# Expert routing in a two-layer decoder: tokens fetched from HBM by index instead of one-hot matmuls

## The chip, the cores and the metric

The kernel runs on one core of a Trainium2 chip (trn2). The metric is the device time of one execution in microseconds (us), lower is better. PE is the matrix engine, PEld its weight loads, DVE the vector engine, ACT the scalar engine, POOL the GpSimd engine and SP the engine whose queue issues most DMAs.

## What is computed

Two layers of a decoder over 256 tokens of width 1024. Layer 0 has a recurrent block, sparse attention, cross-attention and a dense SwiGLU; layer 1 has a state-space mixer, cross-attention and a top-2-of-8 expert SwiGLU. Only the last part is touched:

```
def moe(h, router, w13, w2):
    logits = (h @ router).astype(jnp.float32)
    top_v, top_i = lax.top_k(logits, TOP_K)
    w = jax.nn.softmax(top_v, axis=-1)
    gate = jnp.sum(jax.nn.one_hot(top_i, N_EXPERTS) * w[..., None], axis=-2)
    y = jnp.zeros_like(h)
    for e in range(N_EXPERTS):
        y = y + gate[..., e:e + 1] * swiglu(h, w13[e], w2[e])
    return y
```

Here h is the RMS-normed x (256 tokens by 1024), w13[e] is 1024 by 7168 and w2[e] is 3584 by 1024, all in f32. The result is added to x.

## The kernel before

**Routing.** In `mo_open` the logits give each token two experts. `mo["pos"]` holds, for every token and expert, the token's place among that expert's tokens (1000 is added where it was not chosen), and `mo["gate"]` its weight. An expert works on 128 places. If any expert has more than 128 tokens, a branch at the end (`overflow`) does the rest; it is not entered here.

**Weights.** Each expert has 42 weight pieces of 128 by 2048 f32 (1 MB): 28 of w13 and 14 of w2. The class `Stream` loads them in a fixed order on SP's queue (L208), into 14 buffers in several pools (raw, kv, hl, m_yy). A piece is split in two halves of 1024 columns: ACT copies a rounded high part `wh` (L222), DVE subtracts for the low part `wl` (L225). There are three buffers of `wh` and `wl`. A product is three matmuls, high by high, high by low and low by high (L431, L432, L433). When a piece has been split, its load buffer is free and SP issues the next load.

**Expert loop.** For each expert e and each of seven column blocks c, the steps are four pieces of w13 (`mo_up`, i = 0 to 3, 12 matmuls each), with the transposes of the previous block's hidden values (`mo_tr`, L2029) after i = 0, and then two pieces of w2 for the previous block (`mo_w2`, 12 matmuls each). The end of an expert's w2 therefore falls into block c = 0 of the next expert, where `mo_comb` stands.

**Tokens into an expert.** After (c, i) = (1, 3) `onehot` builds a 0/1 matrix `mo_D` (tokens by places) for the next expert. `x3` holds the normed tokens as three bf16 parts that add up to f32. In blocks 2 to 5, after i = 1 and i = 3, `gather` runs for one of eight column groups k: six bf16 matmuls of 128 columns (L1987), an ACT copy with the norm's gain (L1992) and a DVE subtraction (L1993), into `mo_x0` or `mo_x1` in turn.

**Outputs back to tokens.** After (6, 2) `onehot_T` transposes `mo_D` (two PE transposes, L2003; one ACT copy, L2005). `mo_comb` splits the expert's output from PSUM (two ACT copies, two DVE subtractions, L427 and L428). One and two heavy steps later four pairs of 512-column matmuls (L2066, L2067) bring it back into token order, and DVE adds it to X with the gate as factor (L2069, four times). For the last expert this is the tail of the kernel, with `dump` storing X.

The order of the work on each engine is the order in which the code issues it.

Of the kernel before, what the change touches and what calls it, by code (L numbers as in the profile page):

```python
# [22 lines left out]
D = 1024  # L23
# [79 lines left out]
def pack(inp):  # L103
    a = {k: np.asarray(v) for k, v in inp.items()}
    out = {"x": a["x"][0], "mem": a["mem"][0]}
    par = np.zeros((128, NP_), np.float32)

    def put(k, v):
        par[:, POFF[k][0]:POFF[k][1]] = v
    for l in range(2):  # L110
        for n in ("mix", "cross", "mem", "ffn"):
            put(f"{n}{l}", _cols(a[f"norm_{n}"][l]))
    put("rgw", _cols(a["ev_rg_conv_w"][0]))
    put("rgb", _cols(a["ev_rg_conv_b"][0]))
# [12 lines left out]
    out["cst"], out["cstb"] = _consts()  # L127
    out["grow"] = np.stack([a["norm_mix"][0], a["norm_cross"][0], a["norm_ffn"][0], a["norm_mix"][1],
                             a["norm_cross"][1]])
    out["row"] = np.concatenate([a["od_dt_bias"][0], a["od_a_log"][0], a["od_d_skip"][0],  # L130
                                 a["ev_nsa_gate_b"][0]])[None]
    w_in, od_in = a["ev_w_in"][0], a["od_w_in"][0]
    small = np.concatenate([w_in[:, 4608:4632], od_in[:, 5120:5152], a["moe_router"][0]], 1)
    out["small"] = small.reshape(8, 128, 64).transpose(1, 0, 2).reshape(128, 512)
    out["cw2"] = np.concatenate([a["ev_cmp_k_w2"][0].reshape(2, 128, 128).transpose(1, 0, 2),
                                 a["ev_cmp_v_w2"][0].reshape(2, 128, 128).transpose(1, 0, 2)], 1).reshape(128, 512)
    u = {}
    u["rgx"] = _blocks(w_in[:, 0:1024], 8, 256)
# [27 lines left out]
    return {k: np.ascontiguousarray(v) for k, v in out.items()}  # L166
# [122 lines left out]
def _program(ctx, nc, tc, d, upto):  # L289
# [22 lines left out]
    cstb = dp.tile([128, NB_], BF, name="cstb")  # L312
    sy.dma_start(cst[:, :128], d["cst"][:, :128])
    row = dp.tile([128, 120], F32, name="row")
    gmoe = cp.tile([128, 32], F32, name="gmoe")[:, :8]

    def load_consts():
        sy.dma_start(cst[:, 128:], d["cst"][:, 128:NCK])
# [1569 lines left out]
    def mo_open():  # L1888
# [100 lines left out]
    def gather_out(e, k, ps):  # L1989
# [5 lines left out]
    def gather(e, k):  # L1995
        ps = misc()
        gather_mm(e, k, ps, range(6))
        gather_out(e, k, ps)

    def onehot_T(e):  # L2000
        ps = mo["misc"].tile([128, 1024], BF, name="misc")
# [49 lines left out]
    def mo_comb(e):  # L2051
        def f1():
            oh, ol = (x.rearrange("p k c -> p (k c)").rearrange("p (n c) -> p n c", n=2) for x in mo["xg", e])
            for n in range(2):
                split_to(oh[:, n], ol[:, n], mo["po"][n])

            def f2(t):
                def f():
                    for n in range(2):
                        out(t, n)  # L2060
                return f

            def out(t, n):
                lw = mo["DT", e][:, t * 128:(t + 1) * 128]
                ps = misc()
                mm(ps, lw, oh[:, n], start=True, stop=False)  # L2066
                mm(ps, lw, ol[:, n], start=False, stop=True)  # L2067
                x = X[:, t, n * 512:(n + 1) * 512]
                ve.scalar_tensor_tensor(x, ps, mo["gate"][:, t, e:e + 1], x, op0=OP.mult, op1=OP.add)  # L2069
                if e == NE - 1:  # L2070
                    dump(t, n)
            if e < NE - 1:
                defer(1, f2(0))
                defer(2, f2(1))
            else:
                for n in range(2):
                    for t in range(2):
                        out(t, n)
        add(f1)

    def raw3():
        ST["S"].add_pool(ctx.enter_context(tc.tile_pool(name="raw3", bufs=NRAW3)), NRAW3)
# [1 line left out]
        ST["S"].finish()  # L2084
    add(raw3)
    add(mo_open)
    prev = None
    for e in range(NE):
        for c in range(7):
            for i, (kind, kh) in enumerate(((1, 0), (1, 1), (0, 0), (0, 1))):  # L2090
                mo_up(e, c, kind, kh)
                if i == 0 and prev is not None:
                    mo_tr(*prev)
                if e < 7 and (c, i) == (1, 3):
                    add(lambda e=e: onehot(e + 1))
                if e < 7 and 2 <= c < 6 and i % 2:
                    add(lambda e=e, k=2 * (c - 2) + i // 2: gather(e + 1, k))
                if (c, i) == (6, 2):
                    add(lambda e=e: onehot_T(e))
            if prev is not None:  # L2100
                final = (e, c) == (NE - 1, 6)
                for i in range(2):
                    if final and i:
                        add(lambda: ST["S"].limit(2))
                    mo_w2(*prev, i)
                if final:
                    mo_tr(e, c)
                    add(lambda: ST["S"].limit(3))
                if prev[1] == 6:
                    mo_comb(prev[0])  # L2110
            prev = (e, c)
    for i in range(2):
        mo_w2(*prev, i)
# [3 lines left out]
    def overflow():  # L2117
        n = nc.values_load(mo["cnti"][0:1, 0:1], min_val=0, max_val=256)
        MW.close()
        with tc.If(n > 128), tc.tile_pool(name="ovf", bufs=1) as op_:  # L2120
            D2 = op_.tile([128, 2, 128], BF, name="o_D")
            D2T = op_.tile([128, 256], F32R, name="o_DT")
            p2 = op_.tile([128, 2], F32, name="o_p")
            xg = op_.tile([128, 8, 128], F32, name="o_xg")
            sg = op_.tile([128, 512], F32, name="o_sg")
            hd = op_.tile([128, 512], F32, name="o_hd")
# [9 lines left out]
            for e in range(NE):  # L2136
# [6 lines left out]
                for k in range(8):  # L2143
                    ps = misc()[:, :128]
                    for i in range(6):
                        t, b = divmod(i, 3)
                        mm(ps, mo["x3"][b][:, t, k * 128:(k + 1) * 128], D2[:, t], start=i == 0, stop=i == 5)
                    sc.activation(xg[:, k], ps, AF.Copy, scale=gmoe[:, k:k + 1])
# [50 lines left out]
```

## Time and profile before

| | |
|---|---|
| median of 3 runs | 1796.58 us (1796.31 to 1799.18) |
| the profiled execution | 1799.66 us |
| its span in the profile | 1797.8 us, granted clock 0.989 |
| PE busy, instructions | 1739.1 us, 9381 |
| DVE, ACT, POOL busy | 1409.7, 1172.8, 311.5 us |
| moved by DMA | 478.63 MB, mean 266 GB/s |

The span is from the first to the last instruction; the execution's own time has about 2 us around it. The first expert begins at 802.77 us and the last matmul of all starts at 1788.43 us, so the expert stage is over half of the span. Matmuls overlap one another in the pipeline: the profile shows 0.39 us for one of 512 columns, while they start 0.23 us apart. The chain of waits counts each piece up to the start of the next and is what the times per matmul are read from.

### The profile page before, as it was taken

The numbers are of one execution on the slowest core, as the hardware profiler recorded it, in microseconds if no ns is written. First come the engines' busy times: TensorE is split into PE (matmuls) and PEld (weight loads), VectorE is DVE, ScalarE is ACT, GpSimd is POOL, SyncE is SP. The second block draws the span as 40 slices with busy tenths as digits, with TensorE's granted clock in tenths as the row PEclk, the third lists the DMA queues.
The fourth block names the chain that finished last, engine by engine and source line by source line (L and its number), as shares of the span: only waits on it lengthen the run. The fifth ranks groups of instructions, "written<-read, shape, count | busy, mean of one in ns | idle before, by whom it ended". The sixth has DMA issues, their size and how long they took to land.

```text
span 1797.8 us, 24661 instructions
## 1 busy us (share of the span) xinstructions
PE 1739.1 (97%) x9381; PEld 1453.1 (81%) x9384; DVE 1409.7 (78%) x1727; ACT 1172.8 (65%) x1686; POOL 311.5 (17%) x158
## 2 busy tenths in 40 slices
PE   7999999999998999989999999999999999999997
PEld 6797677899988787768888888888888888888885
DVE  6686756433358898568999899999999998999986
ACT  5646546544444655467787777777777777777774
POOL 4333132444435344230000000000000000000000
PEclk9999999999999999999999999999999999999999
DMA  8555243455563243559999999999999999999970
GB/s 302 214 213 188 85 161 120 181 174 187 193 218 119 99 158 109 232 209 350 358 369 352 352 355 363 362 348 355 361 359 357 368 353 356 357 360 366 356 304 26
DMA packets 71791, 478.63 MB, mean 266 GB/s; under 512 B 10864, under 2 KB 11376, under 8 KB 14448
## 3 DMA queue, kind: packets, MB, share of 16 engines
q1 hardware_dynamic: 67968, 474.36, 70.7%
q10 hardware_dynamic: 3696, 2.62, 0.5%
q8 instruction: 75, 1.23, 0.3%
q14 instruction: 52, 0.43, 0.1%
HBM read 475.90 MB, written 1.05 MB: 265 GB/s over the span
## 4 chain that ended last, share of the span: by engine, by line
PE 81%; DVE 11%; ACT 5%; issue 1%; DMA 1%; POOL 1%; SPq 0%; ACTq 0%; DVEq 0%; POOLq 0%
PE gu L431 11%; PE gu L433 11%; PE gu L432 11%; PE out L431 6%; PE out L433 6%; PE out L432 6%; PE acc L433 5%; PE acc L431 5%; PE acc L432 5%; PE aux L433 2%; PE aux L432 2%; PE aux L431 2%; DVE wl L225 1%; PE misc L2029 1%; PE misc L1987 1%
## 5 line engine op out<-in xcount | busy, mean ns | idle before, releaser
L225 DVE TENSOR_TENSOR wl<-raw,wh 128x1024 fp32r<-128x1024 f32 x619 | 746.3, 1243 | 136.6 <-ACT wh L222 132.5
L222 ACT ACTIVATE wh<-raw 128x1024 fp32r<-128x1024 f32 (+1 forms) x722 | 723.4, 1054 | 149.3 <-PE out L433 52.2
L225 POOL TENSOR_TENSOR wl<-raw,wh 128x1024 fp32r<-128x1024 f32 (+1 forms) x103 | 258.8, 2518 | 311.0 <-ACT wh L222 282.9
L431 PE MATMUL gu<-wh,mo_x0h 128*128 128x512 f32 x448 | 179.4, 400 | 0.0
L431 PE MATMUL gu<-wh,mo_x1h 128*128 128x512 f32 x448 | 179.0, 400 | 0.0
L431 PE MATMUL out<-wh,m_xsT 128*128 128x512 f32 x448 | 177.2, 396 | 0.7 <-ACT m_xsT L427 0.7
L433 PE MATMUL gu<-wh,mo_x0l 128*128 128x512 f32 x448 | 174.9, 390 | 0.0
L433 PE MATMUL gu<-wh,mo_x1l 128*128 128x512 f32 x448 | 174.9, 390 | 0.0
L433 PE MATMUL out<-wh,m_xsT 128*128 128x512 f32 x448 | 174.7, 390 | 0.0
L432 PE MATMUL gu<-wl,mo_x0h 128*128 128x512 f32 x448 | 174.7, 390 | 0.0
L432 PE MATMUL gu<-wl,mo_x1h 128*128 128x512 f32 x448 | 174.6, 390 | 0.0
L432 PE MATMUL out<-wl,m_xsT 128*128 128x512 f32 x448 | 174.4, 389 | 0.0
L431 PE MATMUL acc<-hh,wh 128*128 128x256 f32 x416 | 122.3, 294 | 0.7 <-DVE m_M L810 0.7
L432 PE MATMUL acc<-hl,wh 128*128 128x256 f32 x416 | 119.5, 287 | 0.5 <-DVE hl L428 0.5
L433 PE MATMUL acc<-hh,wl 128*128 128x256 f32 x416 | 119.1, 286 | 0.0
L432 PE MATMUL aux<-hl,wh 128*128 128x256 f32 x352 | 99.9, 284 | 1.3 <-DVE hl L428 1.3
L431 PE MATMUL aux<-hh,wh 128*128 128x256 f32 x352 | 99.8, 284 | 0.3 <-ACT hh L427 0.3
L433 PE MATMUL aux<-hh,wl 128*128 128x256 f32 x352 | 99.8, 283 | 0.0
L433 PEld LDWEIGHTS gu<-wh,mo_x0l 128*128 128x128 f32 x448 | 84.1, 188 | 18.6
L433 PEld LDWEIGHTS gu<-wh,mo_x1l 128*128 128x128 f32 x448 | 84.1, 188 | 18.5
L433 PEld LDWEIGHTS out<-wh,m_xsT 128*128 128x128 f32 x448 | 84.1, 188 | 18.4 <-DVE m_xsT L428 0.4
L431 PEld LDWEIGHTS out<-wh,m_xsT 128*128 128x128 f32 x448 | 84.1, 188 | 17.4 <-ACT m_xsT L427 0.9
(429 smaller groups left out, 3408.9 us busy)
## 6 DMA issues: line engine op xcount, KB each, us to landing
raw<-m SPq DMA_DIRECT2D x265, 1024.0 KB, 6.0
raw<-wd SPq DMA_DIRECT2D x110, 1024.0 KB, 4.8
m_yy<-m SPq DMA_DIRECT2D x24, 1024.0 KB, 6.0
kv<-m SPq DMA_DIRECT2D x24, 1024.0 KB, 5.8
hl<-m SPq DMA_DIRECT2D x23, 1024.0 KB, 5.7
X<-x SPq DMA_DIRECT2D x4, 256.0 KB, 5.1
raw<-wd SPq DMA_DIRECT2D x2, 512.0 KB, 8.3
rg_gw<-wd ACTq DMA_DIRECT2D x1, 1024.0 KB, 11.4
```

Of the source, the lines that this page charges most:

```text
L222: nc.scalar.activation(h[:, a:b], r[:, a:b], AF.Copy)
L225: (nc.gpsimd if eng else nc.vector).tensor_tensor(l[:, a:b], r[:, a:b], h[:, a:b].bitcast(F32), op=OP.subtract)
L431: mm(ps, wh, xh, start=first, stop=False)
L432: mm(ps, wh, xl, start=False, stop=False)
L433: mm(ps, wl, xh, start=False, stop=last)
L1987: mm(ps[:, :128], mo["x3"][b][:, t, k * 128:(k + 1) * 128], mo["D", e][:, t], start=i == 0, stop=i == 5)
L2029: pe.transpose(ps[:, j * 128:(j + 1) * 128], mo["hd", e, c][:, j * 128:(j + 1) * 128], ident)
```

## The change

Tokens and outputs go through HBM. After `mo_open`, the new step `normed` lets POOL multiply X by each token's norm factor and the gain, into f32 rows, and stores them in a DRAM tile `dx`. For experts 1 to 7 `gather_in` computes the token number of each of the 128 places (two matmuls with one column, `mo_D` as weights), and POOL issues an indexed DMA of 128 rows of 4 KB into the buffer `m_y`. After (4, 1) and (4, 3) `gather_tr` transposes them on PE, four transposes at a time, and splits the result as before in high and low part. Expert 0 is still gathered by one-hot matmuls inside `mo_open`.

For experts 0 to 6 `mo_store` takes the place of `mo_comb`: ACT copies the two output banks into SBUF, and POOL stores the 128 rows in the DRAM tile `do`. `choices` (15 small DVE operations in expert 0) computes where each token's two rows lie. In expert 7, after (2, 1) and (4, 1), `rows_out` fetches two rows per token by index for one half of the tokens, and after (4, 0) and (6, 0) `rows_add` adds them to X with their gates. Expert 7 itself keeps `onehot_T` and `mo_comb`.

```
+        for t in range(2):
+            gp.tensor_copy(rs_moe[:, t:t + 1], N["f1"].rs[t])
...
+    def normed():
+        g = m["o"].tile([128, D], F32, name="m_y")
+        gp.dma_start(g, d["grow"][5:6].to_broadcast([128, D]))
...
+        xn = hp.tile([128, 2, D], F32, name="hh")
+        mo["dx"] = dram.tile([T, D], F32, name="dx")
+        for t in range(2):
+            for c in range(2):
+                s = slice(c * 512, (c + 1) * 512)
+                gp.tensor_scalar(xn[:, t, s], X[:, t, s], rs_moe[:, t:t + 1], None, op0=OP.mult)
+                gp.tensor_tensor(xn[:, t, s], xn[:, t, s], g[:, s], op=OP.mult)
+            gp.dma_start(mo["dx"][t * 128:(t + 1) * 128], xn[:, t])
+
+    def rows_in(D_, tok, ix):
+        ps = misc()
+        for t in range(2):
+            mm(ps[:, :1], D_[:, t], tok[:, t:t + 1], start=t == 0, stop=t == 1)
+        ve.tensor_copy(ix, ps[:, :1])
+        rows = m["o"].tile([128, D], F32, name="m_y")
+        gp.indirect_dma_start(rows, None, mo["dx"][:, :], bass.IndirectOffsetOnAxis(ap=ix, axis=0))
+        return rows
...
+    def gather_tr(e, c):
+        ps = misc()
+        for j in range(4):
+            k = c * 4 + j
+            pe.transpose(ps[:, j * 128:(j + 1) * 128], mo["rows"][:, k * 128:(k + 1) * 128], ident)
+        xh, xl = (x[:, c * 4:c * 4 + 4].rearrange("p k c -> p (k c)") for x in mo["xg", e])
+        split_to(xh, xl, ps)
...
-            if e < NE - 1:
-                defer(1, f2(0))
-                defer(2, f2(1))
...
+    def mo_store(e):
+        def f():
+            if e == 0:
+                mo["st"] = hp.tile([128, 2, D], F32, name="hh")
+            o = mo["st"][:, e % 2]
+            for n in range(2):
+                sc.activation(o[:, n * 512:(n + 1) * 512], mo["po"][n], AF.Copy)
+            gp.dma_start(mo["do"][e * 128:(e + 1) * 128], o)
+        add(f)
...
+    def rows_out(t):
+        mo["back"] = [m["o"].tile([128, D], F32, name="m_y"),
+                      mo["st"][:, 1]]
+        for j in range(2):
+            gp.indirect_dma_start(mo["back"][j], None, mo["do"][:, :],
+                                  bass.IndirectOffsetOnAxis(ap=mo["ci"][:, j, t:t + 1], axis=0))
+
+    def rows_add(t):
+        for j in range(2):
+            ve.scalar_tensor_tensor(X[:, t], mo["back"][j], mo["cg"][:, j, t:t + 1], X[:, t],
+                                    op0=OP.mult, op1=OP.add)
...
-                if e < 7 and 2 <= c < 6 and i % 2:
-                    add(lambda e=e, k=2 * (c - 2) + i // 2: gather(e + 1, k))
-                if (c, i) == (6, 2):
+                if e < 7 and (c, i) == (2, 1):
+                    add(lambda e=e: gather_in(e + 1))
+                if e < 7 and c == 4 and i % 2:
+                    add(lambda e=e, h=i // 2: gather_tr(e + 1, h))
+                if (e, c, i) == (0, 3, 0):
+                    add(choices)
+                if (e, c, i) == (7, 6, 2):
                     add(lambda e=e: onehot_T(e))
+                if e == 7 and (c, i) in ((2, 1), (4, 1)):
+                    add(lambda t=c // 2 - 1: rows_out(t))
+                if e == 7 and (c, i) in ((4, 0), (6, 0)):
+                    add(lambda t=c // 2 - 2: rows_add(t))
...
-                    mo_comb(prev[0])
+                    mo_store(prev[0])
```

The change moves instructions, and three places show how (lines of the changed kernel are one to some tens higher). ACT in block c = 4 of expert 0, before; `wh` is a split, `mo_sg` a silu, `m_xsT` the copy after `mo_tr`, `mo_x0h` a gather copy:

```order
L427 ACTIVATE m_xsT<-misc 128x512
L222 ACTIVATE wh<-kv 128x1024 x2
L2019 ACTIVATE mo_sg<-gu 128x512
L1992 ACTIVATE mo_x0h<-misc,gmoe 128x128
L222 ACTIVATE wh<-raw 128x1024 x4
L1992 ACTIVATE mo_x0h<-misc,gmoe 128x128
L222 ACTIVATE wh<-raw 128x1024 x2
```

The same place in the changed kernel:

```order
L429 ACTIVATE m_xsT<-misc 128x512
L223 ACTIVATE wh<-kv 128x1024 x2
L2056 ACTIVATE mo_sg<-gu 128x512
L429 ACTIVATE mo_x1h<-misc 128x512
L223 ACTIVATE wh<-raw 128x1024 x4
L429 ACTIVATE mo_x1h<-misc 128x512
L223 ACTIVATE wh<-raw 128x1024 x2
```

Two copies of 512 columns stand where two of 128 stood; the six other small copies of blocks 2, 3 and 5 are gone. DVE in block c = 4 of expert 7, in the changed kernel (`X<-m_y` and `X<-hh` are `rows_add`):

```order
L2059 TENSOR_TENSOR mo_sg<-mo_sg,gu 128x512
L226 TENSOR_TENSOR wl<-raw,wh 128x1024 x6
L430 TENSOR_TENSOR m_xsT<-misc,m_xsT 128x512
L2150 SCALAR_TENSOR_TENSOR X<-m_y,mo_cg,X 128x1024
L2150 SCALAR_TENSOR_TENSOR X<-hh,mo_cg,X 128x1024
L226 TENSOR_TENSOR wl<-kv,wh 128x1024 x2
```

Two operations of 1024 columns stand between the splits there and once more in block 6; before, expert 7 had four of 512 columns in block 0. POOL, which has no instruction in the expert loop before, in the changed kernel from the start of the loop:

```order
L1994 TENSOR_TENSOR hh<-hh,m_y 128x512
L1995 DMA dx<-hh 128x1024
L1993 TENSOR_SCALAR hh<-X,gmoe 128x512
L1994 TENSOR_TENSOR hh<-hh,m_y 128x512
L1993 TENSOR_SCALAR hh<-X,gmoe 128x512
L1994 TENSOR_TENSOR hh<-hh,m_y 128x512
L1995 DMA dx<-hh 128x1024
L2003 DMA m_y<-dx,mo_ix 128x1024
L2114 DMA do<-hh 128x1024
L2003 DMA m_y<-dx,mo_ix 128x1024
L2114 DMA do<-hh 128x1024
```

Eight elementwise operations come first (four of each kind), then a fetch and a store in turn, seven of each, and four fetches in expert 7.

## Rows read from the trace of the kernel before

**Rows 1.** The page: busy times, and PE's busy tenths in 40 slices.
```profile
PE 1739.1 (97%) x9381; PEld 1453.1 (81%) x9384; DVE 1409.7 (78%) x1727; ACT 1172.8 (65%) x1686; POOL 311.5 (17%) x158
...
PE   7999999999998999989999999999999999999997
```

**Rows 2.** One window: length, busy us (count) by engine, clock, DMA share, GB/s.
```profile
830.00:1740.00 910.00, 910.00 (x4345) 743.38 (x4344) 837.37 (x836) 698.39 (x804) 0.00 (x0) 1.00 0.95 359
```

**Rows 3.** Groups by line and shape, 1000 to 1600 us.
```profile
L225 DVE TENSOR_TENSOR wl<-raw,wh 128x1024 fp32r<-128x1024 f32 x322 | 379.4, 1221 | 31.1 <-ACT wh L222 28.4
L222 ACT ACTIVATE wh<-raw 128x1024 fp32r<-128x1024 f32 x321 | 322.2, 1054 | 57.3 <-PE out L433 32.5 <-PE gu L433 24.8
L431 PE MATMUL gu<-wh,mo_x0h 128*128 128x512 f32 x288 | 115.2, 400 | 0.0
...
L427 ACT ACTIVATE m_xsT<-misc 128x512 fp32r<-128x512 f32 x34 | 20.4, 599 | 36.5 <-PE misc L2029 36.5
...
L2069 DVE SCALAR_TENSOR_TENSOR X<-misc,mo_gate,X 128x512 f32<-128x512 f32 x20 | 14.0, 743 | 0.0
```

**Rows 4.** Waits of SP's queue.
```profile
SPq L208 <- DVE wl L225: 1096.2, 374, 16.5
```

**Rows 5.** Chain, expert 2 (1041.9 to 1165.3 us): shares by line, one piece.
```profile
by line: PE gu L431 21.0%; PE gu L433 20.7%; PE gu L432 20.7%; PE out L431 10.5%; PE out L433 10.5%; PE out L432 10.3%; PE misc L2029 2.5%; PE misc L1987 2.3%; PE misc L2066 0.7%; PE misc L2067 0.7%; PE misc L2003 0.1%
...
1044.85 0.44 PE misc L2029 x4
```

**Rows 6.** Chain, pieces around one gather: start, us, what.
```profile
1013.10 0.23 PE gu L433
1013.33 0.35 PE misc L1987 x6
1013.68 0.29 PE gu L431
```

**Rows 7.** Chain, pieces around the transposes of `mo_tr`, expert 3.
```profile
1168.11 0.44 PE misc L2029 x4
1168.55 0.24 PE gu L431
```

**Rows 8.** Windows of 10 us in which DMA was nearly full.
```profile
730.00:740.00 10.00, 9.66 (x46) 7.57 (x45) 6.84 (x11) 5.48 (x8) 3.90 (x2) 1.00 0.99 415
...
860.00:870.00 10.00, 10.00 (x52) 8.16 (x51) 9.26 (x10) 6.67 (x8) 0.00 (x0) 1.00 0.98 343
...
930.00:940.00 10.00, 10.00 (x48) 8.29 (x47) 9.82 (x11) 8.13 (x10) 0.00 (x0) 1.00 1.00 397
...
1720.00:1730.00 10.00, 10.00 (x46) 8.29 (x45) 9.47 (x10) 7.48 (x8) 0.00 (x0) 1.00 0.99 396
```

**Rows 9.** Timeline: SP's last loads, ACT's last split.
```profile
1737.48 2.60 SPq L208 DMA_DIRECT2D raw<-m  x2
...
1779.19 2.00 ACT L222 ACTIVATE wh<-raw 128x1024 fp32r<-128x1024 f32 x2
```

**Rows 10.** A window of 10 us after the last load.
```profile
1750.00:1760.00 10.00, 10.00 (x46) 8.28 (x45) 9.41 (x10) 8.07 (x10) 0.00 (x0) 1.00 0.01 2
```

**Rows 11.** Timeline of DVE and POOL, 660 to 690 and 770 to 815 us.
```profile
661.68 2.53 DVE L1607 SCALAR_TENSOR_TENSOR m_xsT<-m_th,m_y 128x256 f32<-128x256 f32 x1
...
685.04 0.41 DVE L1607 SCALAR_TENSOR_TENSOR m_xsT<-m_th,m_y 128x256 f32<-128x256 f32 x1
...
773.60 3.49 DVE L225 TENSOR_TENSOR wl<-raw,wh 128x1024 fp32r<-128x1024 f32 x3
...
661.48 2.46 POOL L225 TENSOR_TENSOR wl<-raw,wh 128x1024 fp32r<-128x1024 f32 x1 [5.17 <-ACT wh L222]
...
667.49 3.03 POOL L1667 TENSOR_TENSOR m_y<-m_xs,row 128x512 f32<-128x512 f32 x2
...
773.73 5.56 POOL L225 TENSOR_TENSOR wl<-raw,wh 128x1024 fp32r<-128x1024 f32 x1 [6.80 <-ACT wh L222]
```

**Rows 12.** DMA issues of the page: size and us to landing.
```profile
raw<-m SPq DMA_DIRECT2D x265, 1024.0 KB, 6.0
```

More of the change, by code (lines that the diff above doesn't have):

```diff
@@ L15 @@
 I32 = mybir.dt.int32
+U32 = mybir.dt.uint32
 AF = mybir.ActivationFunctionType
@@ L128, in pack @@
     out["grow"] = np.stack([a["norm_mix"][0], a["norm_cross"][0], a["norm_ffn"][0], a["norm_mix"][1],
-                             a["norm_cross"][1]])
+                             a["norm_cross"][1], a["norm_ffn"][1]])
     out["row"] = np.concatenate([a["od_dt_bias"][0], a["od_a_log"][0], a["od_d_skip"][0],
@@ L314, in _program @@
     row = dp.tile([128, 120], F32, name="row")
-    gmoe = cp.tile([128, 32], F32, name="gmoe")[:, :8]
+    gm = cp.tile([128, 32], F32, name="gmoe")
+    gmoe, rs_moe = gm[:, :8], gm[:, 8:10]
     def load_consts():
@@ L1802, in _program @@
     mo = {}
+    dram = ctx.enter_context(tc.tile_pool(name="dram", bufs=1, space=bass.MemoryType.DRAM))
     add(mb_close2)
@@ L1973, in mo_open, with gather_in @@
         S.advance()
+    def normed():
+        g = m["o"].tile([128, D], F32, name="m_y")
+        gp.dma_start(g, d["grow"][5:6].to_broadcast([128, D]))
+        tk32 = mo["w2"].tile([128, 64], I32, name="mo_ti", bufs=1)[:, :2]
+        tk = mo["tok"] = mo["w2"].tile([128, 64], BF, name="mo_tok", bufs=1)[:, :2]
+        mo["ix"] = mo["w2"].tile([128, 32], U32, name="mo_ix", bufs=1)
+        gp.iota(tk32, pattern=[[128, 2]], base=0, channel_multiplier=1)
+        gp.tensor_copy(tk, tk32)
+        xn = hp.tile([128, 2, D], F32, name="hh")
[14 more added lines that the diff above has]
+        return rows
+    def gather_in(e):
+        mo["rows"] = rows_in(mo["D", e], mo["tok"], mo["ix"][:, e:e + 1])
+    def gather_tr(e, c):
[5 more added lines that the diff above has]
+        split_to(xh, xl, ps)
     def misc():
@@ L1993, in gather_out @@
         ve.scalar_tensor_tensor(xl[:, k], ps[:, :128], gk, xh[:, k].bitcast(F32), op0=OP.mult, op1=OP.subtract)
[L1995 to L1998, printed above, removed]
     def onehot_T(e):
@@ L2055, in f1 @@
                 split_to(oh[:, n], ol[:, n], mo["po"][n])
[L2057 to L2061, printed above, removed]
             def out(t, n):
@@ L2069, in out @@
                 ve.scalar_tensor_tensor(x, ps, mo["gate"][:, t, e:e + 1], x, op0=OP.mult, op1=OP.add)
-                if e == NE - 1:
-                    dump(t, n)
-            if e < NE - 1:
-                defer(1, f2(0))
-                defer(2, f2(1))
[L2075 to L2078, printed above, removed]
-        add(f1)
+                dump(t, n)
+            for n in range(2):
+                for t in range(2):
+                    out(t, n)
@@ new lines, in mo_comb, with choices @@
+        add(f1)
+    def mo_store(e):
[3 more added lines that the diff above has]
+            o = mo["st"][:, e % 2]
+            for n in range(2):
+                sc.activation(o[:, n * 512:(n + 1) * 512], mo["po"][n], AF.Copy)
+            gp.dma_start(mo["do"][e * 128:(e + 1) * 128], o)
+        add(f)
+    def choices():
+        n = NE - 1
+        p = mo["w2"]
+        mo["do"] = dram.tile([n * 128, D], F32, name="do")
+        mo["cg"] = p.tile([128, 32], F32, name="mo_cg", bufs=1)[:, :4].rearrange("p (j t) -> p j t", j=2)
+        mo["ci"] = p.tile([128, 32], U32, name="mo_ci", bufs=1)[:, :4].rearrange("p (j t) -> p j t", j=2)
+        v, q, w = (p.tile([128, 32], F32, name=f"mo_c{k}", bufs=1)[:, :2 * n].rearrange("p (t e) -> p t e", t=2)
+                   for k in "vqw")
+        r = p.tile([128, 32], F32, name="mo_cr", bufs=1)[:, :4].rearrange("p (j t) -> p j t", j=2)
+        pos, gate = (mo[k][:, :, :n] for k in ("pos", "gate"))
+        base = C("iota")[:, :n].unsqueeze(1).to_broadcast([128, 2, n])
+        ve.tensor_scalar(v, pos, 128.0, None, op0=OP.is_lt)
+        ve.scalar_tensor_tensor(q, base, 128.0, pos, op0=OP.mult, op1=OP.add)
+        ve.scalar_tensor_tensor(q, q, 1.0, v, op0=OP.add, op1=OP.mult)
+        ve.tensor_tensor(v, v, gate, op=OP.mult)
+        ve.tensor_reduce(r[:, 0], q, op=OP.max, axis=AX.X)
+        ve.tensor_reduce(r[:, 1], q, op=OP.add, axis=AX.X)
+        ve.tensor_tensor(r[:, 1], r[:, 1], r[:, 0], op=OP.subtract)
+        for j in range(2):
+            ve.tensor_tensor(w, q, r[:, j].unsqueeze(2).to_broadcast([128, 2, n]), op=OP.is_equal)
+            ve.tensor_tensor(w, w, v, op=OP.mult)
+            ve.tensor_reduce(mo["cg"][:, j], w, op=OP.add, axis=AX.X)
+            ve.tensor_scalar(mo["ci"][:, j], r[:, j], -1.0, 0.0, op0=OP.add, op1=OP.max)
@@ new lines, in rows_out @@
+    def rows_out(t):
[5 more added lines that the diff above has]
+    def rows_add(t):
+        for j in range(2):
+            ve.scalar_tensor_tensor(X[:, t], mo["back"][j], mo["cg"][:, j, t:t + 1], X[:, t],
+                                    op0=OP.mult, op1=OP.add)
@@ L2086, in _program @@
     add(mo_open)
+    add(normed)
     prev = None
@@ L2123, in overflow @@
             p2 = op_.tile([128, 2], F32, name="o_p")
+            t32 = op_.tile([128, 2], I32, name="o_t32")
+            tok = op_.tile([128, 2], BF, name="o_tok")
+            ix = op_.tile([128, 1], U32, name="o_ix")
+            gp.iota(t32, pattern=[[128, 2]], base=0, channel_multiplier=1)
+            gp.tensor_copy(tok, t32)
             xg = op_.tile([128, 8, 128], F32, name="o_xg")
@@ L2142, in overflow @@
                 sc.activation(D2T, ps[:, :256], AF.Copy)
[L2143 to L2148, printed above, removed]
+                rows = rows_in(D2, tok, ix)
+                for c in range(2):
+                    ps = misc()
+                    for j in range(4):
+                        k = c * 4 + j
+                        pe.transpose(ps[:, j * 128:(j + 1) * 128], rows[:, k * 128:(k + 1) * 128], ident)
+                    sc.activation(xg[:, c * 4:c * 4 + 4].rearrange("p k c -> p (k c)"), ps, AF.Copy)
                 po = [mo["out"].tile([128, 512], F32, name="out") for _ in range(2)]
```

## Prediction

> **What bounds the kernel now.** I read the page first: PE's digits are 9 in every slice of the second half but the last [rows 1]. That alone says little, since matmuls overlap, so I read the window of the expert stage next: from 830 to 1740 PE is busy all the time at full granted clock, DVE for 837 of 910 us, 92%, ACT for 77%, DMA 0.95 of its time at 359 GB/s, POOL not at all [rows 2]. Four resources are nearly full, and the question is which ends the waits of the others. The groups by line answer it: PE's matmuls have no idle time before them, ACT's splits were idle 57.3 us until PE's matmuls ended, DVE's 31.1 us until ACT [rows 3], and SP's queue stood 1096 us until DVE had freed a load buffer [rows 4]. So PE bounds the stage: it frees `wh`, ACT fills it, DVE follows, and the load follows DVE. The chain of waits through one expert is PE alone [rows 5]. The first piece of `mo_tr` lies at 1044.85 in expert 2 and at 1168.11 in expert 3 [rows 5, 7], so an expert takes 123.26 us. What shortens PE's list shortens the stage, as long as the others keep up.
>
> **What PE loses.** In the chain a matmul of 512 columns takes 0.23 us. A gather of six small matmuls takes 0.35, and the next large one 0.29 instead of 0.23, since its weights come late [rows 6]: 0.41 in all, times 8 is 3.28 us per expert. The way back is 8 matmuls of 0.23, 1.84 us; by shares, 1.4% of 123.3 us is 1.7 [rows 5]. `onehot_T` is 0.1% of the expert, 0.12, and some 0.06 more in the matmul behind it: 0.2. Together 5.3 us per expert.
>
> **What PE gains.** `gather_tr` is two groups of four transposes, the same as `mo_tr`: 0.44 and 0.01 in the next matmul, 0.45 [rows 7], so 0.9 per expert. The two matmuls with one column in `rows_in` have no row. They can't cost less than nothing, and hardly more than a group of four transposes, 0.45; I take 0.2, like the two transposes of `onehot_T`, which also are two loads of 128 by 128 with little behind them. Net 5.3 - 1.1 = 4.2 us per expert. Gathers go for experts 1 to 7, and way back and `onehot_T` for 0 to 6, so seven times each: **29.4 us off PE's list**.
>
> **ACT and DVE.** Seven gathers lose eight small ACT copies and DVE subtractions each and gain two of 512 columns (ACT 0.60 [rows 3]); the way back loses four DVE additions of 0.743 each and two subtractions, and the two ACT copies stay as the store's. Both engines get lighter. What counts is the order: the splits can run two pieces ahead of PE (three buffers), 2 x 12 x 0.23 = 5.5 us, of which ACT's two halves take 2.1 and DVE's last half behind them 1.2 (1054 and 1221 ns [rows 3]), so some 2 us of lead is left. An ACT copy behind transposes waits about 1.1 us (36.5 us over 34 [rows 3]) and takes 0.6, and the splits behind it start that much later: 1.7, within the lead, as `mo_tr` shows in every block without idle time on PE. In block 4 the changed order puts three such copies into four steps. I cost that at nothing; were the lead used up, 0.6 us for each of two copies (2.1 + 1.7 for a piece whose matmuls and transposes take 3.2) in seven experts would be 8.4 us.
>
> `rows_add` puts two DVE operations of 1024 columns before a split, twice. Their price lies between a split of that width, 1.22, and two additions of 512, 1.49 [rows 3]: 2.4 to 3.0 us against a lead of 2. I take 0.5 each, **1 us**, with 0 and 2 as ends. The 15 small operations of `choices` have lead enough, spread over one piece: nothing.
>
> **The start: `normed` on POOL.** Eight POOL operations of 128 by 512 run beside DVE's first splits. A POOL operation of that size took 1.5 us when DVE was at work (two in 3.03 [rows 11]). The same rows show what happens to DVE: an operation that takes 0.41 alone took 2.53 and ended as a POOL operation did, 661.68 + 2.53 against 661.48 + 2.46. So DVE stood while POOL worked. It can be the other way round: at 773.6 three splits took 1.16 each, nothing lost, and POOL's operation 5.56 instead of 2.46. From below it costs nothing then, and from above 8 x 1.5 = 12 us of DVE's time; less 2 of lead and 0.3 for each of some six pieces in that time (a piece takes PE 2.72 and DVE 2.4) that is 8 on PE. I take **2.5 us**, in the lower half, since the splits stand back to back there and mostly come first. The Trainium skill (SBUF — State Buffer, "SBUF: two separate sides") calls the port pair of DVE and GpSimd an exclusive lock, held for the whole instruction, also against DVE operations with two SBUF inputs. By that rule whoever starts first wins each time, so the cost lies between the same two ends; the trace agrees that the loser stands for the whole of the other's operation.
>
> **The other queues.** SP's order of loads does not change. POOL's queue has a fetch and a store per expert, and nobody else waits for POOL. The fetch is issued after (2, 1) and needed after (4, 1), two blocks later, 2 x 17 = 34 us; a load of 1 MB lands in 6.0 us [rows 12], so a fetch of half that size has five times that as cover. The fetches for `rows_add` have about 30 us.
>
> **The transfers.** An expert loads 42 x 1.049 = 44.0 MB. The change adds 0.52 of store and 0.52 of fetch to each of seven, 2.1 of fetches in expert 7 and 1.6 at the start (the gain and `dx`): 11 MB. With PE at 119 us per expert, DMA must move 45.1 MB in it, 379 GB/s, where it now moves 359. Is there room? Share 0.95 at 359 would be 378 at 1.0 [rows 2]; windows of 10 us at 0.98 to 1.0 reached 415, 397 and 396, and one 343 [rows 8]. And there is a store of time: the last load is issued at 1740 and the DMAs are idle from 1750 on, while ACT splits the last piece at 1779 [rows 9, 10]. Loads land about 30 us ahead of their use. From 830 to 1740 pass 910 x 0.359 = 327 MB, and some 2 behind them; with 11 more they must be there by 1779 - 29 = 1750, so 340 MB in 920 us: from **370 GB/s** on the gain is whole, and below it PE waits at the end.
>
> **The sum.** 29.4 - 2.5 - 1 = 26 us. The profiled execution took 1799.7 (its span 1797.8 and 1.9 around it), so 1773.7; the median of the runs lies 3.1 lower, 1796.6, and I forecast **1770.6 us** for the median. The bounds: the PE terms with nothing lost, 1767, and a little less if the small matmuls are free; with 8 at the start, 2 for `rows_add` and some of block 4, 1780. Chance 0.74.
>
> **Rival 1: transfers bind.** If 359 GB/s is all that the DMAs give over so long a time, 11 MB more cost 31 us of DMA, the 30 us of lead are eaten, and the last load comes when it is needed today: 1796, no gain. For it: 910 us passed at 359, and one nearly full window gave only 343 [rows 2, 8]. Against: SP waited for buffers, so the DMAs were never asked for more, and three windows went well beyond. A ceiling of 364 would cost half the gain (340 / 0.364 = 934, 14 us more than 920), 1784. The Trainium skill (DMA: Bandwidth & Descriptors, "Where 436 GB/s comes from") says just this: that about 358 GB/s per core is the limit of transfers between HBM and SBUF. By that rule this rival would be the forecast. The windows at 396 to 415 contradict it as a hard limit. Chance 0.1 for a loss of half the gain or more, of which 0.05 within 0.2% of before.
>
> **Rival 2: the splits bind.** If the lead in block 4 is smaller than I think, PE waits there in each expert: 8.4 us given back, 1779, and with a late start up to 1785. For it: DVE at 92%. Against: DVE loses more work per expert than PE does, and ACT is idle for a quarter of the time [rows 2]. Chance 0.09.
>
> **Rival 3, slower: fetches come late.** PE's transposes of `gather_tr` stand in line ahead of all its later matmuls. If an indexed fetch takes over 34 us, PE stops for the rest in each of seven experts; from 34 + 4.2 = 38 us on the kernel is slower than before. At 45 us it would be 7 x 11 - 26 = 51 us slower, 1847. For it: no indexed DMA is in the trace, its addresses must be read and made into 128 transfers on POOL, and POOL can be held up by DVE, as at 773.7 [rows 11]. Against: whole loads of twice the size take 6.0 us, so it needs six times that. Chance 0.05; with slower ways of rival 1 (mixed reads and writes below 355 GB/s) 0.07.
>
> That the change does not do what it says is hardly open: the order of instructions shows the small matmuls gone.
>
> **Chances.** Runs of this kernel differ by about 0.2%, 3.6 us. Faster: 0.74 + 0.09 + 0.05 = 0.88; same 0.05; slower 0.07. The range from 1764 to 1785 holds the forecast and rival 2 whole, and leaves out 0.17.
>
> **What would show it.** The distance of the same `mo_tr` in experts 2 and 3 should be 119.0 instead of 123.26; `gather_tr` 0.44 per group without idle time before it; fetches landing in under 15 us; DMA near 379 GB/s with the last load still 15 us or more ahead of its use; PE's waits, if any, between 810 and 835 us, on DVE. I am wrong if PE shows idle time in every expert, on m_y (rival 3), on wh from a DMA (rival 1) or on wl (rival 2).

## The result and the profile after

The changed kernel takes **1771.21 us** (median of 4 runs, 1767.92 to 1772.36), the kernel before 1796.44 beside it (4 runs, 1796.1 to 1799.18): a ratio of 0.9852 with a 95% interval of 0.9839 to 0.9864, so 25 us faster. The profiled execution took 1771.26 us (its span is 1769.5) and lies on the median; that of before lies 3.2 us above its median, so between the two profiles the difference is 28.4.

The page first: the row of busy times, and DMA's busy tenths in 40 slices. The first answers to [rows 1].

```profile
PE 1709.3 (97%) x9048; PEld 1436.1 (81%) x9048; DVE 1384.9 (78%) x1669; ACT 1162.3 (66%) x1637; POOL 346.7 (20%) x191
...
DMA  8555244455563243558999999999999999999980
```

Two windows of the changed kernel (columns as in [rows 2]): the start of the expert stage, and the stretch in which the loads run.

```profile
800.00:830.00 30.00, 27.34 (x124) 22.45 (x123) 25.73 (x30) 20.55 (x26) 21.59 (x17) 0.93 0.82 297
830.00:1710.00 880.00, 880.00 (x4013) 726.46 (x4013) 805.71 (x778) 689.37 (x755) 17.50 (x18) 1.00 0.99 381
```

From 830 on PE is still busy all the time at full granted clock; DMA moves 381 GB/s instead of 359. In the first 30 us PE is busy for 27.34 (before 29.93): that is the one place where the change cost something. The groups by line, 1000 to 1600 us, answer to [rows 3]: ACT's splits wait for PE as before, PE's matmuls for nothing.

```profile
L226 DVE TENSOR_TENSOR wl<-raw,wh 128x1024 fp32r<-128x1024 f32 x333 | 391.0, 1220 | 37.3 <-ACT wh L223 36.9
L223 ACT ACTIVATE wh<-raw 128x1024 fp32r<-128x1024 f32 x334 | 335.1, 1053 | 62.0 <-PE out L435 36.1 <-PE gu L435 25.8
L433 PE MATMUL gu<-wh,mo_x0h 128*128 128x512 f32 x307 | 122.1, 398 | 0.0
```

The chain of waits of the changed kernel, pieces of experts 2 and 3 (start, us, what). L2066 is `mo_tr`, L2000 the pair of `rows_in`, L2013 `gather_tr`; the first and last row answer to [rows 5, 7].

```profile
1040.38 0.43 PE misc L2066 x4
...
1077.23 0.04 PE misc L2000 x2
1077.27 0.34 PE gu L433
...
1111.01 0.44 PE misc L2013 x4
1111.45 0.24 PE gu L433
...
1159.24 0.44 PE misc L2066 x4
```

The same `mo_tr` now comes back after 118.86 us, before after 123.26: 4.40 us per expert. A group of `gather_tr` costs 0.44 and 0.01 in the matmul behind it, `rows_in` 0.04 and 0.11.

Where the span's 28.3 us lie, from the first matmul of an expert to that of another in both traces. These are the first matmuls of experts 0 and 1, before and after:

```profile
802.77 0.48 PE L431 MATMUL gu<-wh,mo_x0h 128*128 128x512 f32 x1
...
918.70 0.39 PE L431 MATMUL gu<-wh,mo_x1h 128*128 128x512 f32 x1
```

```profile
801.14 0.47 PE L433 MATMUL gu<-wh,mo_x0h 128*128 128x512 f32 x1
...
918.65 0.39 PE L433 MATMUL gu<-wh,mo_x1h 128*128 128x512 f32 x1
```

| stretch | before | after | difference |
|---|---|---|---|
| up to expert 0 | 802.77 | 801.14 | -1.6 |
| expert 0 | 115.93 | 117.51 | +1.6 |
| experts 1 to 6 | 739.61 | 713.12 | -26.5 |
| expert 7 to the end of the span | 139.5 | 137.7 | -1.8 |

The code up to expert 0 is hardly changed, and the runs of one kernel differ by more than 1.6; the rest is the change. Expert 7 gains just the way back of expert 6, 1.84. Expert 0 should have gained about 2.4 (eight gathers and `onehot_T` against two `gather_tr` and `rows_in`) and lost 1.6: in this trace its **start costs 4 us**. Here is DVE beside POOL (timeline of the changed kernel; PE's row is the first `mo_tr`), and behind it DVE's same four splits and the same `mo_tr` in the kernel before.

```profile
809.75 1.29 POOL L1994 TENSOR_TENSOR hh<-hh,m_y 128x512 f32<-128x512 f32 x1 [1.87 <-DMA m_y<-grow]
809.89 7.15 DVE L226 TENSOR_TENSOR wl<-raw,wh 128x1024 fp32r<-128x1024 f32 x4 [1.82 <-ACT wh L223]
811.02 3.59 POOL L1993 TENSOR_SCALAR hh<-X,gmoe 128x512 f32<-128x512 f32 x1
...
816.96 0.67 DVE L2059 TENSOR_TENSOR mo_sg<-mo_sg,gu 128x512 f32<-128x512 f32 x1
817.56 3.44 DVE L226 TENSOR_TENSOR wl<-raw,wh 128x1024 fp32r<-128x1024 f32 x2
817.69 0.86 PE L2066 MATMUL misc<-cst,mo_sg 128*128 128x128 f32 x4 [2.67 <-DVE mo_sg L2059]
```

```profile
811.44 4.63 DVE L225 TENSOR_TENSOR wl<-raw,wh 128x1024 fp32r<-128x1024 f32 x4 [2.17 <-ACT wh L222]
...
816.72 0.66 PE L2029 MATMUL misc<-cst,mo_sg 128*128 128x128 f32 x4
```

Four splits took 7.15 instead of 4.63, `mo_sg` behind them came late, and PE stood 2.67 us, where its row of before shows no wait. POOL in turn stood for DVE: its operation takes 1.58 us at 816.93 and 3.59 here. Then something the prediction did not have, in the chain of the same kernel:

```profile
818.56 0.43 PE gu L433
...
821.12 0.43 PE gu L433
821.54 0.23 PE gu L434
```

Seven matmuls start 0.43 apart instead of 0.23. The window of that stretch shows the clock:

```profile
818.50:821.50 3.00, 3.00 (x9) 2.32 (x8) 3.00 (x3) 2.49 (x3) 2.92 (x3) 0.51 0.90 313
```

The granted clock is 0.51 there, and from 822 on 1.00: after the stall PE ran at its lower level, 1.2 GHz, and then at 2.4 again. The seven matmuls (1.4 us) and the transposes (0.86 us, where the same four took 0.66 before) are 1.6 us on top of the stall.

### The profile page after: what moved, and what is told of

Same layout as the page of the kernel before. It is cut to its first block, busy times and chain, and to the rows that moved or that the text cites. A ratio compares the mean times of both kernels' runs of the same rounds, so it can differ in the third digit from the quotient of the medians.

```text
span 1769.5 us, 23965 instructions
## 1 busy us (share of the span) xinstructions
PE 1709.3 (97%) x9048; PEld 1436.1 (81%) x9048; DVE 1384.9 (78%) x1669; ACT 1162.3 (66%) x1637; POOL 346.7 (20%) x191
## 4 chain that ended last, share of the span: by engine, by line
PE 81%; DVE 11%; ACT 4%; issue 2%; POOL 1%; DMA 0%; SPq 0%; ACTq 0%; DVEq 0%; POOLq 0%
PE gu L433 11%; PE gu L435 11%; PE gu L434 11%; PE out L433 6%; PE out L435 6%; PE out L434 6%; PE acc L435 5%; PE acc L433 5%; PE acc L434 5%; PE aux L434 2%; PE aux L435 2%; PE aux L433 2%; DVE wl L226 2%; PE misc L2066 1%; DVE m_y L848 1%
## 5 line engine op out<-in xcount | busy, mean ns | idle before, releaser
L2114 POOL DMA_DIRECT2D do<-hh x7 | 4.0, 568 | 661.5 <-ACT hh L2113 661.5
L433 PEld LDWEIGHTS out<-wh,m_xsT 128*128 128x128 f32 x448 | 84.1, 188 | 18.1 <-ACT m_xsT L429 0.9
```

What stands on the lines that cost most here:

```text
L433: mm(ps, wh, xh, start=first, stop=False)
L2114: gp.dma_start(mo["do"][e * 128:(e + 1) * 128], o)
```

## The experiments

**One half of the change at a time.** `gather_only` keeps the fetch and sends outputs back by one-hot matmuls:

```
...
-                    mo_store(prev[0])
+                    mo_comb(prev[0])
```

`scatter_only` keeps the way back and gathers by one-hot matmuls. The output copy has one buffer of its own there, and one load buffer goes for it (13 instead of 14):

```
...
-    add(normed)
...
-                if e < 7 and (c, i) == (2, 1):
-                    add(lambda e=e: gather_in(e + 1))
-                if e < 7 and c == 4 and i % 2:
-                    add(lambda e=e, h=i // 2: gather_tr(e + 1, h))
+                if e < 7 and 2 <= c < 6 and i % 2:
+                    add(lambda e=e, k=2 * (c - 2) + i // 2: gather(e + 1, k))
```

> Tokens fetched by index as in the change, outputs of all experts brought back by one-hot matmuls as before. Theory (PE's list of work sets the stage, and POOL's arithmetic at the start costs some 3.7 us): an expert takes 123.26 - (3.28 - 0.90 - 0.20) = 121.1 us, and the time is 1796.4 - 15.3 + 3.7 = 1785 us. Rival (the splits on DVE and ACT set the pace, and the change helped by making their lists shorter): DVE loses 8 x 0.35 - 2 x 0.69 = 1.4 us per expert here, so 121.9 us per expert and 1790.

> Outputs of experts 0 to 6 stored and fetched by index as in the change, tokens gathered by one-hot matmuls as before (so no arithmetic on POOL at the start). To make room the stream has 13 load buffers instead of 14, and the store one buffer instead of two. Theory: 1.84 + 0.2 = 2.04 us less on PE in each of seven experts, 121.2 us per expert and 1796.4 - 14.3 = 1782 us, with no wait at the start; together with the gather alone the two gains add up to the whole change's. Rival (splits): DVE loses 4 x 0.74 + 2 x 0.68 = 4.3 us per expert, 119 us per expert and 1766.

Measured: `gather_only` 1783.91 us (1781.24 to 1785.63), ratio 0.9924 (0.9908 to 0.9941); `scatter_only` 1782.92 (1781.64 to 1784.75), ratio 0.9921 (0.9905 to 0.9938). The chains, `mo_tr` of experts 2 and 3, first `gather_only` and then `scatter_only`:

```profile
1042.58 0.44 PE misc L2066 x4
...
1163.48 0.44 PE misc L2066 x4
```

```profile
1041.85 0.44 PE misc L2071 x4
...
1163.07 0.44 PE misc L2071 x4
```

The distances are 120.90 and 121.22. Against the whole change the fetch alone lacks 2.04 us per expert, the way back and `onehot_T` as they were costed (1.84 + 0.2); the way back alone lacks 2.36, the gathers less `gather_tr` and `rows_in` (3.28 - 0.9 - 0.2 = 2.18 as costed). So the two halves add up, and each is worth what its instructions take on PE. The time of `gather_only` also has the start's cost in it, which `scatter_only` has not: expert 0 takes 117.67 us in the one and 115.78 in the other.

**The removed matmuls put back on PE alone.** `pe_back` is the changed kernel with matmuls of the removed shapes and number, at their old places, whose results nobody reads:

```
...
+                if e < 7 and 2 <= c < 6 and i % 2:
+                    add(lambda e=e: dummy_gather(e + 1))
+                if e > 0 and c == 1 and i < 2:
+                    add(lambda e=e: dummy_out(e))
+                if e < 7 and (c, i) == (6, 2):
+                    add(lambda e=e: dummy_T(e))
```

> The changed kernel with the removed matmuls put back on PE alone, their results unused: eight times six bf16 matmuls of 128 columns, eight matmuls of 512 columns, two transposes per expert. ACT and DVE keep their shorter lists. Theory (PE sets the stage): 118.85 + 5.3 = 124.2 us per expert and 1771.2 + 37 = 1808 us, slower than the kernel before, since gather_tr and the start stay. Rival (ACT's and DVE's shorter lists made the gain): 1771 to 1775.

Measured: 1811.0 us (1808.62 to 1811.42), ratio 1.0081 (1.0064 to 1.0098), slower than before. Its chain:

```profile
1046.12 0.44 PE misc L2084 x4
...
1170.61 0.44 PE misc L2084 x4
```

124.49 us per expert, 5.63 over the changed kernel (5.3 as costed, times seven 37 and 39). PE's list is all of the gain.

**Small work put back on ACT and DVE.** `vec_back` adds one ACT copy and two DVE operations of 128 columns at each of the eight places of the gathers:

```
...
+                if e < 7 and 2 <= c < 6 and i % 2:
+                    add(dummy_small)
```

> The changed kernel with ACT and DVE work of about the removed length put back, no work on PE: at each of the eight old gather places of an expert two DVE operations and one ACT copy of 128 by 128 into a scratch tile, some 5.5 us of DVE and 2.9 us of ACT per expert. Theory (PE sets the stage, the splits have 2 to 3.5 us of lead): 1771 us, at most 3 more if the lead runs out somewhere. Rival (DVE's list sets the pace): up to 7 x 5.5 = 38 us more, 1795 to 1809.

Measured: 1769.74 us (1767.39 to 1771.82), ratio 0.9849 (0.9833 to 0.9866): no difference from the changed kernel. A window of it, and its `mo_tr`:

```profile
1000.00:1600.00 600.00, 600.00 (x2739) 495.23 (x2738) 564.33 (x601) 477.73 (x555) 7.87 (x10) 1.00 0.99 380
```

```profile
1038.85 0.44 PE misc L2074 x4
...
1157.71 0.44 PE misc L2074 x4
```

DVE is busy 564 of 600 us, 94% (553 before, 548 in the changed kernel), and the distance stays 118.86. By these busy times ACT has back all of the 1.3 us per expert that the change took off it, DVE only 3.2 of 5.1. But DVE is left with less idle time than in the kernel before, and PE loses nothing. Rival 2 falls.

**The start.** `raw_dx` stores X itself, so POOL has no arithmetic beside DVE; norm and gain are left out for experts 1 to 7. `dve_normed` computes the right rows on DVE, in two operations after (2, 0) and (2, 2), with the fetch for expert 1 after (3, 1) and `choices` in block 5:

```
-                gp.tensor_scalar(xn[:, t, s], X[:, t, s], rs_moe[:, t:t + 1], None, op0=OP.mult)
-                gp.tensor_tensor(xn[:, t, s], xn[:, t, s], g[:, s], op=OP.mult)
...
+            ve.scalar_tensor_tensor(xn[:, t], X[:, t], rs_moe[:, t:t + 1], g, op0=OP.mult, op1=OP.mult)
```

> The changed kernel without the eight elementwise operations on POOL: X is stored in dx as it is, so experts 1 to 7 get tokens without norm and gain (the norm is left out). Theory (POOL's operations hold up DVE's splits at the start, PE waits some 3 us and then runs at half clock for a while): no wait and no dip of the clock after 803 us, expert 0 shorter by 3 to 4 us, 1767.5 us. Rival (the wait comes from the first loads or from the order of DVE's own work): as the change, 1771.

> The changed kernel with norm and gain applied by DVE, one operation of 128 by 1024 per half of the tokens, after (2, 0) and (2, 2) of expert 0, where the splits have a lead of 2 us or more; the first fetch goes out after (3, 1), choices in block 5. POOL only issues DMAs. Theory: each operation takes 1.25 us of DVE and fits the lead, no wait on PE at the start: 1767.5 us. Rival (any extra work on DVE near the start costs its time): 1767.5 + 2.5 = 1770 or as the change, 1771.

Measured: `raw_dx` 1766.57 us (1765.49 to 1767.98), ratio 0.983 (0.9817 to 0.9844); `dve_normed` **1765.36** (1764.86 to 1768.37), ratio 0.9829 (0.9816 to 0.9842), some 6 us below the changed kernel (the two ratios' intervals just touch). PE's first matmul of expert 0 and of expert 1, and DVE's first added operation, in the timeline of `dve_normed`:

```profile
798.77 0.48 PE L433 MATMUL gu<-wh,mo_x0h 128*128 128x512 f32 x1
...
912.14 0.39 PE L433 MATMUL gu<-wh,mo_x1h 128*128 128x512 f32 x1
...
831.52 1.27 DVE L1991 SCALAR_TENSOR_TENSOR hh<-X,gmoe,m_y 128x1024 f32<-128x1024 f32 x1
```

Expert 0 takes 113.37 us instead of 117.51, and the same 113.37 in `raw_dx`: the start's 4.1 us are back. The other 2.4 us between the two profiles lie ahead of expert 0 (798.77 against 801.14), where the runs of one kernel differ as much. DVE pays 2 x 1.27 us of its own and PE waits for nothing; in the changed kernel POOL's eight operations took DVE 0.43 + 2.52 + 1.09 + 1.09 = 5.1 us by standing in the way of ten splits.

The start's cost is not one number. Its code is the same in eight traces, and they fall into two groups. In five (the changed kernel, `gather_only`, `traffic`, `traffic20`, `late_fetch`) POOL's second operation begins 0.05 to 0.24 us ahead of DVE's run of four splits, as in the rows above; the splits take 7.06 to 7.24 us, PE stands 2.57 to 2.75 us, and matmuls 0.43 apart follow. In `pe_back`, `vec_back` and `late_gap` DVE's run begins first. The timeline of `late_gap`:

```profile
809.33 6.15 DVE L226 TENSOR_TENSOR wl<-raw,wh 128x1024 fp32r<-128x1024 f32 x4 [2.25 <-ACT wh L223]
809.38 2.34 POOL L1994 TENSOR_TENSOR hh<-hh,m_y 128x512 f32<-128x512 f32 x1 [0.94 <-DMA m_y<-grow]
```

In these three the splits take 6.15 us, PE stands 1.66 or 1.67 us, and the granted clock stays at 1.00 behind it. Expert 0 takes 115.84 us in `vec_back` and 115.64 in `late_gap`, so the start costs 2.3 to 2.5 us there instead of 4.1. In all eight the cost goes with which engine began first, by some tenths of a microsecond; how often each comes in the timed runs is not shown.

**More transfers.** `traffic` has POOL read 10 pieces of 0.5 MB more in each of experts 1 to 6, `traffic20` 20 (`i % 2` in place of `i == 1`), into the buffers of the output copies, where nobody reads them:

```
+    def extra(c):
+        for j in range(2):
+            gp.dma_start(mo["st"][:, j], d["m13"][0, c, j][:, 0:1024])
...
+                if 1 <= e < 7 and 1 <= c < 6 and i == 1:
+                    add(lambda c=c: extra(c))
```

> The changed kernel with ten more reads of 0.5 MB in each of experts 1 to 6, on POOL's queue into the idle store buffers, unused: 50.3 MB per expert instead of 45.1. Theory (PE sets the stage, the DMAs are nearly full at 380 to 389 GB/s and can give about 390): 129 us per expert are needed, 10 more than PE takes, times 6, less the 28 us by which loads run ahead: 1800 us, 1795 to 1810, and SP's loads then land just before their use. If the DMAs can give 415 GB/s or more, 121.3 us per expert, all within the lead: 1771. If 370 is their end: 136 us, 1846.

> The changed kernel with 20 extra reads of 0.5 MB in each of experts 1 to 6, twice the traffic run's. Theory: the DMAs end at the 425 GB/s that the traffic run reached. An expert then moves 45.1 + 10.5 = 55.6 MB, 131 us at 425 against the 118.9 that PE needs; six experts fall 72 us behind, of which the lead of the loads takes 20 to 28, so 45 to 55 us more than the changed kernel, 1815 to 1825, a few more if PE loses its clock in the waits; DMA at 425 GB/s in the windows and PE waiting on wh, ACT on raw. Rival: 425 was only what was asked for and the ceiling is above 440: under 1800. Second rival: POOL's queue cannot issue 20 reads in an expert's time in two buffers, so fewer bytes per microsecond are asked for and the fetches come late: PE waits on m_y, not on wh.

Measured: `traffic` 1769.88 us (1769.03 to 1770.68), ratio 0.9849 (0.9834 to 0.9864): nothing lost. Its theory, 1800 us, was missed; what came is the case named beside it, 415 GB/s or more. `traffic20` took 1822.44 us (1819.24 to 1823.67), ratio 1.013 (1.0114 to 1.0147), as its theory had it. One window of each:

```profile
1000.00:1600.00 600.00, 600.00 (x2739) 495.33 (x2738) 548.14 (x520) 469.86 (x514) 34.56 (x60) 1.00 1.01 424
```

```profile
1000.00:1600.00 600.00, 578.50 (x2556) 458.98 (x2555) 508.32 (x485) 437.55 (x481) 58.22 (x104) 1.00 1.01 425
```

424 GB/s with PE full, and 425 with PE starved: that is what the DMAs give here. The DMA share was 0.99 at 381 and 1.01 at 424, so a share near 1 did not mean that they were at their end; a load of 1 MB lands in 7.4 us, 11.3 and 26.1 in the three kernels from 1000 to 1600. In `traffic20` the groups by line show the sign of a bound by transfers, ACT's splits waiting for loads (115.4 us where the changed kernel has 62.0, and from another cause):

```profile
L223 ACT ACTIVATE wh<-raw 128x1024 fp32r<-128x1024 f32 x311 | 312.4, 1053 | 115.4 <-DMA raw<-m 90.7 <-PE out L435 9.2 <-PE gu L435 8.2
```

Rival 1 falls with room to spare. The Trainium skill (HBM Reference, "Specifications (TRN2)") says that a core that streams alone reaches about 425 GB/s, the 358 being its share when both cores of a pair stream; on this one core the two windows agree.

**The fetch late.** `late_fetch` issues it after (3, 3), which leaves 11 us:

```
-                if e < 7 and (c, i) == (2, 1):
+                if e < 7 and (c, i) == (3, 3):
                     add(lambda e=e: gather_in(e + 1))
```

> The changed kernel with each indexed fetch issued after (3, 3) instead of (2, 1), needed after (4, 1) as before: 48 matmuls of 0.23 us later, 11 us of cover instead of 34. Theory (a fetch takes about 10.5 us from its index matmul to the transposes: 1 for the cast, 1 on POOL, 9.2 to landing): no wait or up to 1 us per expert, 1771 to 1778. Rival (fetches need 20 us or more, and the change's cover hid it): 9 us and more per expert, 1834 or above.

Measured: 1779.97 us (1779.44 to 1783.33), ratio 0.9911 (0.9896 to 0.9927), a little above its theory's range. A fetch lands 9.1 us after its issue in the changed kernel, so 11 us should nearly do, and experts 1 to 6 take 714.0 us together instead of 713.1. The loss is in expert 0, which takes 127.3 us. Timeline there, and the fetch of the next expert:

```profile
862.50 6.89 DVE L226 TENSOR_TENSOR wl<-raw,wh 128x1024 fp32r<-128x1024 f32 x6
...
862.87 7.44 POOL L2003 DMA_INDIRECT m_y<-dx,mo_ix  x1 [40.01 <-DVE mo_ix L2001]
...
869.31 0.68 DVE L430 TENSOR_TENSOR m_xsT<-misc,m_xsT 128x512 fp32r<-128x512 f32 x1
...
878.05 1.11 PE L2013 MATMUL misc<-cst,m_y 128*128 128x128 f32 x4 [6.67 <-DMA m_y<-dx,mo_ix]
...
990.17 1.71 POOL L2003 DMA_INDIRECT m_y<-dx,mo_ix  x1 [45.23 <-DVE mo_ix L2001]
```

DVE's six splits ran until 869.39; POOL's issue, begun among them, ended 0.92 us later, and the fetch landed 15.1 us after its issue was begun. PE waited 6.67 and then ran its next stretch at the lower clock:

```profile
878.50:884.00 5.50, 5.50 (x16) 4.43 (x15) 3.05 (x3) 2.49 (x3) 0.00 (x0) 0.50 0.11 43
```

Twelve matmuls at 0.43 and four transposes in 1.11 cost 3.1 us more; 6.7 + 3.1 is the 9.8 that expert 0 lost. `late_gap` tells whether DVE held POOL up: the same late fetch, with `choices` moved away so that DVE has no backlog there.

```
-                if (e, c, i) == (0, 3, 0):
+                if (e, c, i) == (0, 5, 0):
                     add(choices)
```

> The late fetch once more (issued after (3, 3), cover 11 us), with the 15 small DVE operations of choices in block 5 of expert 0 instead of block 3. In the late fetch POOL's issue of the first indexed DMA took 7.44 us, 862.87 to 870.31, while DVE ran six splits and a subtraction back to back until 869.99; in experts 1 to 6, where DVE paused after two splits, it took 1.71. Theory: POOL can write the fetch's descriptors only when DVE pauses. Without choices DVE has no backlog there, the issue takes 1.7 to 4 us, PE waits under 2 us for the first fetch, and the time is 1770 to 1774. Rival: the first late fetch is slow for another reason of its own (first use, the state of the queues), DVE has no part in it: issue near 7.4 us again, PE waits 6 to 7 us in expert 0, time 1779 to 1781.

Measured: 1770.6 us (1768.28 to 1771.59), ratio 0.9845 (0.9829 to 0.9862): the 9 us are gone. The issue, in its timeline:

```profile
860.76 2.35 DVE L226 TENSOR_TENSOR wl<-raw,wh 128x1024 fp32r<-128x1024 f32 x2
...
861.13 1.76 POOL L2003 DMA_INDIRECT m_y<-dx,mo_ix  x1 [33.52 <-DVE mo_ix L2001]
...
863.37 2.36 DVE L226 TENSOR_TENSOR wl<-raw,wh 128x1024 fp32r<-128x1024 f32 x2 [0.27 <-ACT wh L223]
```

Here it stood behind one split of 1.22 us and took 1.76. In the changed kernel it begins just ahead of DVE's split and takes 0.98, though the split runs over it:

```profile
959.91 0.98 POOL L2003 DMA_INDIRECT m_y<-dx,mo_ix  x1 [22.77 <-DVE mo_ix L2001]
959.99 2.36 DVE L226 TENSOR_TENSOR wl<-raw,wh 128x1024 fp32r<-128x1024 f32 x2 [0.35 <-ACT wh L223]
```

So an indexed DMA's issue on POOL waits for a split of DVE that began before it, and with a backlog for the whole run. Why it got in after the first of two splits, and not between the six, stays open. A plain DMA's issue does not wait: in `traffic20` all 120 extra reads were issued in 0.54 to 0.57 us, in the midst of DVE's splits too:

```profile
974.33 2.36 DVE L226 TENSOR_TENSOR wl<-raw,wh 128x1024 fp32r<-128x1024 f32 x2 [0.26 <-ACT wh L223]
974.73 0.54 POOL L2039 DMA_DIRECT2D hh<-m  x1 [6.82 <-DMA hh<-m]
```

The Trainium skill (SBUF — State Buffer, "Who interferes with whom") has a rule that parts the two: a DVE instruction with two inputs in SBUF contends with a GpSimd instruction that reads SBUF, not with one that only writes there. The indexed issue reads its row numbers from SBUF and the plain one reads none; both rows agree with that. That the reading is what waits was not tried by itself.

## Why the prediction was right

The forecast was 1770.6 us, the measurement 1771.21. By its own steps:

- **What bounds the kernel.** PE's list: `pe_back` took the gain away and more, `vec_back` nothing. One reading behind it was too wide: the 1096 us of [rows 4] are SP's waits over the whole kernel; from 830 to 1740 us they are 695.8, which says the same.
- **What PE loses and gains.** 4.2 us per expert forecast, 4.40 measured, 119.0 against 118.86 as the distance. 26.5 in experts 1 to 6, 1.8 in expert 7 and about 2.4 in expert 0 make 30.7 where 29.4 stood. `gather_tr` came out at 0.45 as taken, `rows_in` at 0.15 instead of 0.2.
- **ACT and DVE.** The lead covered the copies of block 4, as costed. `rows_add` was put at 1 us and cost none: its pairs took 1.27 + 1.28 us, within the forecast 2.4 to 3.0, and PE waited for nothing there. The changed kernel has one wait of PE between 800 and 1740 us, the one at 817.69.
- **The start.** This is the term that was mis-sized: 2.5 forecast, 4 in the trace of the changed kernel, within its ends of 0 and 8. (Where DVE's run began first, 2.3 to 2.5 were measured.) The place and the engine were right, between 810 and 835 on DVE, and both engines held each other up as in [rows 11]. Two things were not in the step: PE waited for `mo_sg`, which stands behind the splits, so the lead of the splits did not help; and the stall brought the lower clock, 1.6 of the 4 us.
- **The transfers.** From 370 GB/s on the gain was to be whole; 381 were moved. The lead of the loads stayed: SP issues the last two at 1710.79 and ACT splits the last piece at 1750.83, 40 us later (before 42, [rows 9]). A ceiling near 359 GB/s, on which rival 1 stood, is not there: `traffic` moves 424. The windows at 396 to 415 [rows 8] were the better witness, and still low; 378 from the share of 0.95 was no ceiling either.
- **The fetches.** 9.1 us against a cover of 34. What rival 3 feared, POOL held up by DVE, does exist: `late_fetch` shows it in one expert, an issue of 7.44 us instead of 0.98, which a cover of 34 hides.

The sum by measured terms is 30.7 - 4 = 26.7, where 26 was forecast. The list gave 1.3 us more than forecast and `rows_add` cost 1 less, which the start's 1.5 more nearly cancels: that the time was met to 0.6 us is in part luck, the mechanism is not. The other 1.6 of the 28.3 lie ahead of the experts, within what two runs of one kernel differ by.

## What to carry to other kernels

Where one engine has no idle time, cost a change by what it takes off that engine's list, piece by piece from the chain of waits; then ask only whether the others keep their lead, and put their work back or double it to see. Work given to POOL beside a DVE that is busy is not free: two operations on DVE, placed where it has lead, were cheaper than eight on POOL by 2.3 to 4.1 us, depending on which engine began first. An indexed DMA wants its issue ahead of DVE's next run, or cover enough for the longest one.

## What was not expected of the hardware

- A stall of PE of 2.67 us was followed by 3 us at a granted clock of 0.51, one of 6.67 by 5.5 us or more at 0.50. The lower clock cost 1.6 and 3.1 us on top of the waits. Behind the stalls of 1.67 us in `vec_back` and `late_gap` the clock stayed at 1.00.
- POOL's second operation at the start began 0.14 us ahead of DVE's four splits in the changed kernel, and they took 7.15 us; it began 0.05 us behind them in `late_gap`, and they took 6.15.
- The DMAs' share stood at 0.99 with 381 GB/s and at 1.01 with 424; loads only took longer to land (7.4 and 11.3 us).
- An indexed issue on POOL took 0.98, 1.71 or 7.44 us, by how many splits of DVE it stood behind; a plain one 0.54.
